# A hybrid model's layers on one core: the norm's weight and scale in one instruction behind the power, x's parts side by side, x loaded first, the first MLP chunk by token halves

## Chip, cores and metric

The kernel runs on one core of a Trainium2 chip. The metric is the device time of one execution in microseconds. TensorE (PE) multiplies matrices, VectorE (DVE), ScalarE (ACT) and GpSimd (POOL) work on rows of elements, SyncE (SP) and ACT issue most of the DMAs here. Each engine works through its instructions in the order in which they stand in its program, and waits on semaphores for the others.

## The reference, cut to what matters

```python
D_MODEL, SEQ, DEPTH, NORM_EPS = 1024, 256, 2, 1e-6

def rms_norm(x, w):
    xf = x.astype(jnp.float32)
    xf = xf * lax.rsqrt(jnp.mean(xf * xf, axis=-1, keepdims=True) + NORM_EPS)
    return (xf * w.astype(jnp.float32)).astype(x.dtype)
```

256 tokens of width 1024, all in fp32, pass through two layers, each a mixer (hgrn, dilated attention and a state-space part on slices of one projection) and a "peer" block (product keys choose experts), then an RG-LRU block, an MLP, a sparse-attention block (nsa), a second MLP, and a last norm. Each block is x + block(rms_norm(x, w)), and an MLP is `relu(x @ up)**2 @ down`. The change rewrites the norms, eight ahead of blocks and one at the end.

## The kernel before, in words

The residual x stays in SBUF as two token halves (t = 0, 1) of 128 partitions by 1024, each worked on in two column halves (`HALVES`, j = 0, 1). Every weight chunk of 512 KB (128x1024, fp32) is loaded into a tile `raw` (`load`, L258, SP's queue) and split by `chunk` into two fp32r parts, `hi` (a cast on ACT, L271) and `lo` (raw - hi on DVE, L273). The normed activations are split in the same way into `xh` and `xl`, the two parts of a tile `xx`. A product takes three matmuls: hi with xh, lo with xh, hi with xl. `feat_mm` (L289) takes 256 columns (all tokens) at a time; its first call after a norm does all eight of the first kind, then the eight of the second, then the eight of the third. `feat_cat` (L295, L296), used in the MLPs from the second chunk on, takes hi with xh and xl as one operand of 512 columns, and lo with xh beside it with 256. `tok_mm` (L322) makes the sums with tokens as rows, into four PSUM tiles; its last matmuls (L353) and the additions into x (L356) go token half by token half.

The norm ahead of each block (`norm_T`) goes through these steps:
- `squares`: per token half two squares on ACT (L381) with their sums in `nss`.
- `normed`: per token half two DVE multiplies x * sqrt(D) * w (L390), then `ns` on DVE (L392, sum plus epsilon), its power -1/2 on POOL (L393), and two DVE scalings by it (L398). For t = 0 the output is the tile `norm`, for t = 1 `nxs`.
- eight transposes on PE for each token half (L428), four to a PSUM tile; casts of these to xh on ACT (L435); the subtractions that give xl on DVE (L420).
- keep-warm matmuls of ones (L310) between the transposes of the two halves, in every norm but the first.

A scheduler (the tile framework) orders each engine's instructions. `issue_after` tells it that an instruction is to be issued behind another one. `self.behind` holds such instructions for the next three chunks: hi of the first is issued behind the last square and its lo behind the last scaling, the next two behind the last cast (hi) and the last subtraction (lo).

At the start, ACT's queue loads x, and SP's queue loads the first norm's weights, broadcast to all partitions (512 KB), ahead of the first weight chunks. Functions of setup make small constants meanwhile.

Of the kernel before, what the change touches and what calls it, by code (L numbers as in the profile page):

```python
# [10 lines left out]
F32 = mybir.dt.float32  # L11
# [10 lines left out]
P = 128  # L22
S = 256
# [158 lines left out]
class K:  # L182


    def __init__(self, ctx, tc, a):
# [9 lines left out]
        self.added = self.summed = self.row = None  # L195
# [23 lines left out]
    def load_x(self, src):  # L219
        for t in range(NT):  # L220
            for js in HALVES:
                self.nc.scalar.dma_start(self.x[:, t, js], src[t * P:(t + 1) * P, js])
            if t == 0:
                self.row = self.norm_row("attn_norm", 0)
        self.nc.scalar.dma_start(self.ident, self.a["c_ident"])
# [53 lines left out]
    def feat_mm(self, ps, wh, wl, xh, xl, m=P, kc=KC):  # L279
# [8 lines left out]
        for i, (w, x, k) in enumerate(seq):  # L288
            nc.tensor.matmul(ps, w[:, k], x[:, k], start=i == 0, stop=i == len(seq) - 1)  # L289

    def feat_cat(self, ps, wh, wl, x2, kc=KC):

        nc = self.nc
        for k in range(kc):
            nc.tensor.matmul(ps, wh[:, k], x2[:, :, k], start=k == 0, stop=False)  # L295
            nc.tensor.matmul(ps[:, :S], wl[:, k], x2[:, 0, k], start=False, stop=k == kc - 1)  # L296

    def split_x(self, name):

        x2 = self.stream.tile([P, 2, KC, S], F32R, tag="x2", name=self.nm(name))  # L300
        return x2, x2[:, 0], x2[:, 1]
# [75 lines left out]
    def squares(self, t):  # L377

        ss = self.const.tile([P, 2], F32, tag="nss", name=self.nm("nss"), bufs=2)
        for j, js in enumerate(HALVES):  # L380
            last = self.nc.scalar.activation(self.bank("a"), self.x[:, t, js], AF.Square, accum_out=ss[:, j:j + 1])  # L381
        return ss, last

    def normed(self, t, ss, w, dst, between=lambda: None):
# [3 lines left out]

        for js in HALVES:
            ready = nc.vector.scalar_tensor_tensor(dst[:, js], self.x[:, t, js], math.sqrt(D), w[:, js], op0=OP.mult, op1=OP.mult)  # L390
        with self.issue_after(ready):
            last = nc.vector.scalar_tensor_tensor(r, ss[:, 0:1], D * EPS, ss[:, 1:2], op0=OP.add, op1=OP.add)  # L392
# [3 lines left out]
        with self.issue_after(last):  # L396
            for js in HALVES:
                last = nc.vector.tensor_scalar(dst[:, js], dst[:, js], r, None, op0=OP.mult)  # L398
        return last

    def norm_row(self, wname, wi):
# [4 lines left out]
        return w  # L406

    def norm_T(self, pool, wname, wi):

        nc = self.nc  # L410
        w, self.row = self.row if self.row is not None else self.norm_row(wname, wi), None
# [9 lines left out]

        for t in range(NT):
            sc = self.normed(t, sq[t][0], w, xs[t], (lambda: low(0)) if t else lambda: None)
# [7 lines left out]
            if t == 0 and self.summed is not None:  # L431

                self.keep_warm(4, tr, self.summed)
            for _, b, h in parts[2 * t:]:
                cp = nc.scalar.copy(h, b)  # L435
# [3 lines left out]
        self.behind = [(sq[1][1], sc), (cp, self.lows), (cp, self.lows)]  # L439
# [29 lines left out]
    def setup_first(self):  # L469
# [5 lines left out]
        nc.vector.tensor_tensor(t[:, 0:2], hl[:, 0:2], hl[:, 2:4], op=OP.max)  # L475
# [11 lines left out]
        nc.vector.tensor_scalar(self.cwh, self.cols[:, o:o + 70], 0.5, None, op0=OP.mult)  # L487
        self.qn = c.tile([P, 2], F32, name="qn8")
        nc.vector.tensor_scalar(self.qn, self.col("q_norm", 0, 2), 0.125, None, op0=OP.mult)
# [4 lines left out]
        nc.scalar.activation(self.nega, self.nega, AF.Exp)  # L494
# [8 lines left out]
        nc.tensor.matmul(b[:6, :384], rb, oh, start=True, stop=True)  # L503
# [671 lines left out]
    def setup_second(self):  # L1175
# [97 lines left out]
    def mlp(self, i):  # L1273
        nc, a, tc = self.nc, self.a, self.tc
        v3 = lambda t_: t_.rearrange("p (k m) -> p k m", k=KC)
        with tc.tile_pool(name=f"mlp{i}", bufs=3) as pool:
# [4 lines left out]
            def up(f):  # L1281
# [3 lines left out]
                if f == 0:  # L1285
                    self.feat_mm(b[:, :S], v3(wh), v3(wl), xh, xl)
# [323 lines left out]
```

## Time and profile before

| | us |
|---|---|
| three runs | 2548.58, 2551.44, 2552.85 |
| median | 2551.44 |
| profiled execution, time | 2545.15 |
| profiled execution, span of the core | 2543.4 |
| PE busy | 2493.9 |
| DVE busy | 1875.2 |
| ACT busy | 1230.2 |

The span goes from the first to the last instruction. The mean granted clock of PE over it is 0.991 of full speed. Busy times are sums over the span; engines work beside each other, so they say how full an engine is, not what the end waits for. The busy time of one matmul (0.28 us for 256 columns) overlaps with the next; from one start to the next is less.

### The profile page before, as it was taken

The page shows a single profiled execution, that of the slowest core. Times are in us where ns is not written, and L with a number is a line of the kernel's source. Part 1 is how long each engine was busy: PE and PEld are TensorE (multiplying, and loading weights), DVE is VectorE, ACT ScalarE, POOL GpSimd, SP SyncE. Part 2 cuts the span into 40 slices and gives each one's busy share as a digit, 9 for nine tenths or more (in the row PEclk, how much of TensorE's full clock was granted, in tenths as well). Part 3 has the DMA queues.
Part 4 walks back from the last instruction along what each step waited for, and adds up shares of the span by engine and source line. Part 5 has one row for each costly group of instructions (what it writes and reads, how often), then busy time and mean ns, then how long its engine had stood idle before and what let it go on. Part 6 is the DMA issues. An engine that isn't in the chain of part 4 may idle for free.

```text
span 2543.4 us, 42782 instructions
## 1 busy us (share of the span) xinstructions
PE 2493.9 (98%) x16984; PEld 2159.3 (85%) x16984; DVE 1875.2 (74%) x3309; ACT 1230.2 (48%) x1861; POOL 55.6 (2%) x70
## 2 busy tenths in 40 slices
PE   8999999999999998999999999999999999999998
PEld 6789999988878887889989988878889788886887
DVE  8769969965696557869969955696559766756666
ACT  5544454445534445544454345534447544455544
POOL 2000000000000003000000000000000000000000
PEclk9999999999999998999999999999999999999999
DMA  6334454455545555244554455545555455621554
GB/s 214 104 134 158 176 189 160 156 194 187 174 158 185 195 191 178 95 141 153 179 191 158 158 192 189 174 150 191 196 193 173 167 190 189 202 73 61 192 189 149
DMA packets 122065, 426.17 MB, mean 168 GB/s; under 512 B 14748, under 2 KB 18696, under 8 KB 121736
## 3 DMA queue, kind: packets, MB, share of 16 engines
q1 hardware_dynamic: 120856, 421.79, 48.4%
q8 instruction: 133, 2.18, 0.3%
q10 hardware_dynamic: 1008, 1.64, 0.2%
q14 instruction: 68, 0.56, 0.1%
HBM read 421.83 MB, written 2.24 MB: 167 GB/s over the span
## 4 chain that ended last, share of the span: by engine, by line
PE 82%; DVE 13%; ACT 2%; issue 1%; DMA 1%; POOL 0%; ACTq 0%; POOLq 0%; DVEq 0%
PE psacc L322 40%; PE psa L289 14%; PE psa L295 12%; PE psa L296 6%; DVE lo L273 4%; PE psg L1044 2%; PE psacc L289 2%; DVE tk L940 1%; PE psa L1474 1%; PE psacc L353 1%; DVE si L942 1%; DVE si L939 1%; DVE sv L941 1%; DVE sv L938 0%; PE psacc L428 0%
## 5 line engine op out<-in xcount | busy, mean ns | idle before, releaser
L271 ACT CAST hi<-raw 128x1024 fp32r<-128x1024 f32 (+1 forms) x778 | 811.0, 1045 | 919.8 <-PE psa L289 343.9
L273 DVE TENSOR_TENSOR lo<-raw,hi 128x1024 fp32r<-128x1024 f32 (+1 forms) x778 | 942.5, 1218 | 412.0 <-ACT hi L271 411.3
L289 PE MATMUL psa<-xx,hi 128*128 128x256 f32 x3328 | 602.5, 285 | 4.3 <-ACT xx L435 1.7
L289 PEld LDWEIGHTS psa<-xx,hi 128*128 128x128 f32 x3328 | 515.4, 192 | 8.0 <-ACT xx L435 3.6
L289 PE MATMUL psa<-xx,lo 128*128 128x256 f32 x1664 | 463.1, 284 | 2.0 <-DVE lo L273 1.9
L295 PE MATMUL psa<-xx,hi 128*128 128x512 f32 x1296 | 463.3, 400 | 0.5 <-ACT mr L1287 0.5
L296 PE MATMUL psa<-xx,lo 128*128 128x256 f32 x1296 | 362.7, 280 | 0.0
L289 PEld LDWEIGHTS psa<-xx,lo 128*128 128x128 f32 x1664 | 314.7, 192 | 5.2 <-DVE lo L273 4.6
L322 PE MATMUL psacc<-hi,ch 128*128 128x512 f32 x984 | 306.4, 392 | 0.1
L322 PE MATMUL psacc<-lo,ch 128*128 128x512 f32 x984 | 304.3, 390 | 0.0
L322 PE MATMUL psacc<-hi,cl 128*128 128x512 f32 x984 | 303.6, 389 | 0.3 <-DVE cl L1015 0.2
L295 PEld LDWEIGHTS psa<-xx,hi 128*128 128x128 f32 x1296 | 243.3, 188 | 63.9 <-DVE ca L971 3.8
L296 PEld LDWEIGHTS psa<-xx,lo 128*128 128x128 f32 x1296 | 244.6, 189 | 2.4
L322 PEld LDWEIGHTS psacc<-hi,cl 128*128 128x128 f32 x984 | 184.6, 188 | 40.1 <-DVE cl L1015 1.2
L322 PEld LDWEIGHTS psacc<-lo,ch 128*128 128x128 f32 x984 | 184.7, 188 | 38.7
L322 PEld LDWEIGHTS psacc<-hi,ch 128*128 128x128 f32 x984 | 182.6, 188 | 36.4
L1014 ACT CAST ch<-ca 128x512 fp32r<-128x512 f32 x124 | 76.9, 621 | 139.9 <-PE psacc L322 137.7
L1015 DVE TENSOR_TENSOR cl<-ca,ch 128x512 fp32r<-128x512 f32 x124 | 85.4, 690 | 58.3 <-ACT ch L1014 58.0
L1048 DVE TENSOR_TENSOR ca<-psg,ca 128x512 f32<-128x512 f32 x128 | 82.2, 683 | 16.5 <-PE psg L1044 15.1
L322 PE MATMUL psacc<-hi,xx 128*128 128x512 f32 (+1 forms) x320 | 86.0, 380 | 0.0
L1034 DVE TENSOR_TENSOR pg<-o,selg 128x1024 f16<-128x1024 f16 x128 | 82.4, 682 | 0.0
L322 PE MATMUL psacc<-hi,muh 128*128 128x512 f32 x248 | 78.9, 397 | 0.0
(411 smaller groups left out, 2796.6 us busy)
## 6 DMA issues: line engine op xcount, KB each, us to landing
raw<-in_down SPq DMA_DIRECT2D x256, 512.0 KB, 3.2
raw<-in_up SPq DMA_DIRECT2D x256, 512.0 KB, 3.2
raw<-in_mlp_up SPq DMA_DIRECT2D x64, 512.0 KB, 3.3
raw<-in_mlp_down SPq DMA_DIRECT2D x64, 512.0 KB, 3.3
raw<-in_w_in_t SPq DMA_DIRECT2D x32, 512.0 KB, 3.9
raw<-in_w_in_f SPq DMA_DIRECT2D x22, 512.0 KB, 3.8
raw<-in_w_out SPq DMA_DIRECT2D x16, 512.0 KB, 3.4
raw<-in_w_query SPq DMA_DIRECT2D x16, 512.0 KB, 3.2
```

Of the source, the lines that this page charges most:

```text
L271: nc.scalar.copy(hi, src)
L273: nc.vector.tensor_sub(lo, src, hi)
L289: nc.tensor.matmul(ps, w[:, k], x[:, k], start=i == 0, stop=i == len(seq) - 1)
L295: nc.tensor.matmul(ps, wh[:, k], x2[:, :, k], start=k == 0, stop=False)
L296: nc.tensor.matmul(ps[:, :S], wl[:, k], x2[:, 0, k], start=False, stop=k == kc - 1)
L322: nc.tensor.matmul(acc[t][n][:, :widths[n]], x[:, xs], w[:, off[n]:off[n] + widths[n]], start=first and i == 0, stop=last and i == len(seq ...
L353: self.summed = nc.tensor.matmul(acc[t][j], x_[:, ts_], w_[:, HALVES[j]], start=False, stop=w_ is wl)
L1014: nc.scalar.copy(ch.rearrange("p b t -> p (b t)"), src)
L1015: nc.vector.tensor_sub(cl.rearrange("p b t -> p (b t)"), src, ch.rearrange("p b t -> p (b t)"))
L1034: nc.vector.tensor_tensor(pairs(pg[:, i]), pairs(o1), twice(sg[:, i], 32), op=OP.mult)
L1044: nc.tensor.matmul(bk[:, tt * 64:(tt + 1) * 64], o2[:, tk], pg[:, i, tk], start=i == 0, stop=i == 1)
L1048: nc.vector.tensor_tensor(v, bk.rearrange("p (t i) -> p i t", t=8), v, op=OP.mult)
```

## The change

- `normed` takes the power first; then one DVE instruction per column half makes x * r * w. The squares are scaled by D^-0.5 in place of the factor sqrt(D). For t = 0 the second half is issued behind the last x add. ns of t = 1 is issued behind the multiplies of t = 0.
- All casts to xh are issued behind the last square. Three keep-warm matmuls stand in place of four. hi of the first chunk is issued behind the casts of t = 0.
- `xx` is laid out so that xh and xl of one k stand side by side.
- x is loaded first, t = 0 on SP's queue and t = 1 on ACT's; the first norm's weights come as one row of 1024, which two matmuls with ones spread over the partitions into PSUM (`first_weights`).
- The first chunk of an MLP runs as 48 matmuls of 128 columns (`feat_tiles`), one token half after the other.
- Setup work on DVE, ACT and PE is issued behind the last subtraction, or the last matmul of the first product (most of these places are left out below).

```diff
@@ -217,12 +217,22 @@
         return self.ps.tile([P, 512], F32, tag=tag, name=self.nm("ps" + tag), bufs=bufs)
 
     def load_x(self, src):
-        for t in range(NT):
+        nc = self.nc
+        for t, q in zip(range(NT), (nc.sync, nc.scalar)):
             for js in HALVES:
-                self.nc.scalar.dma_start(self.x[:, t, js], src[t * P:(t + 1) * P, js])
-            if t == 0:
-                self.row = self.norm_row("attn_norm", 0)
-        self.nc.scalar.dma_start(self.ident, self.a["c_ident"])
+                q.dma_start(self.x[:, t, js], src[t * P:(t + 1) * P, js])
+        self.first_row = self.wts.tile([P, D], F32, tag="raw", name="first_row", bufs=4)[0:1]
+        nc.scalar.dma_start(self.ident, self.a["c_ident"])
+        nc.scalar.dma_start(self.first_row, self.a["attn_norm"][0:1, :])
+
+    def first_weights(self):
+
+        w = []
+        for js in HALVES:
+            b = self.bank("acc", 4)
+            self.nc.tensor.matmul(b, self.ones[0:1, :P], self.first_row[:, js], start=True, stop=True)
+            w.append(b)
+        return w
 
     def rstd(self, pool, ss, n, width):
 
@@ -286,19 +296,27 @@
         else:
             seq = [(w, x, k) for k in range(kc) for w, x in ((wh, xh), (wh, xl), (wl, xh))]
         for i, (w, x, k) in enumerate(seq):
-            nc.tensor.matmul(ps, w[:, k], x[:, k], start=i == 0, stop=i == len(seq) - 1)
+            self.last_mm = nc.tensor.matmul(ps, w[:, k], x[:, k], start=i == 0, stop=i == len(seq) - 1)
+
+    def feat_tiles(self, ps, wh, wl, xh, xl, kc=KC):
+
+        for t in range(NT):
+            ts_ = slice(t * P, (t + 1) * P)
+            for w, x in ((wh, xh), (wl, xh), (wh, xl)):
+                for k in range(kc):
+                    self.nc.tensor.matmul(ps[:, ts_], w[:, k], x[:, k, ts_], start=w is wh and x is xh and k == 0, stop=x is xl and k == kc - 1)
 
     def feat_cat(self, ps, wh, wl, x2, kc=KC):
 
         nc = self.nc
         for k in range(kc):
-            nc.tensor.matmul(ps, wh[:, k], x2[:, :, k], start=k == 0, stop=False)
-            nc.tensor.matmul(ps[:, :S], wl[:, k], x2[:, 0, k], start=False, stop=k == kc - 1)
+            nc.tensor.matmul(ps, wh[:, k], x2[:, k], start=k == 0, stop=False)
+            nc.tensor.matmul(ps[:, :S], wl[:, k], x2[:, k, 0], start=False, stop=k == kc - 1)
 
     def split_x(self, name):
 
-        x2 = self.stream.tile([P, 2, KC, S], F32R, tag="x2", name=self.nm(name))
-        return x2, x2[:, 0], x2[:, 1]
+        x2 = self.stream.tile([P, KC, 2, S], F32R, tag="x2", name=self.nm(name))
+        return x2, x2[:, :, 0], x2[:, :, 1]
 
     def keep_warm(self, n, *after):
 
@@ -378,24 +396,23 @@
 
         ss = self.const.tile([P, 2], F32, tag="nss", name=self.nm("nss"), bufs=2)
         for j, js in enumerate(HALVES):
-            last = self.nc.scalar.activation(self.bank("a"), self.x[:, t, js], AF.Square, accum_out=ss[:, j:j + 1])
+            last = self.nc.scalar.activation(self.bank("a"), self.x[:, t, js], AF.Square, scale=D ** -0.5, accum_out=ss[:, j:j + 1])
         return ss, last
 
-    def normed(self, t, ss, w, dst, between=lambda: None):
+    def normed(self, t, ss, w, dst, between=lambda: None, behind=None):
 
         nc = self.nc
         r = self.const.tile([P, 1], F32, tag="ns1", name=self.nm("ns1"), bufs=2)
-
-        for js in HALVES:
-            ready = nc.vector.scalar_tensor_tensor(dst[:, js], self.x[:, t, js], math.sqrt(D), w[:, js], op0=OP.mult, op1=OP.mult)
-        with self.issue_after(ready):
-            last = nc.vector.scalar_tensor_tensor(r, ss[:, 0:1], D * EPS, ss[:, 1:2], op0=OP.add, op1=OP.add)
+        with self.issue_after(behind):
+            last = nc.vector.scalar_tensor_tensor(r, ss[:, 0:1], EPS, ss[:, 1:2], op0=OP.add, op1=OP.add)
         nc.gpsimd.tensor_tensor(r, r, self.mhalf[:, :1], op=OP.pow)
         with self.issue_after(last):
             last = between() or last
         with self.issue_after(last):
-            for js in HALVES:
-                last = nc.vector.tensor_scalar(dst[:, js], dst[:, js], r, None, op0=OP.mult)
+            for j, js in enumerate(HALVES):
+
+                with self.issue_after(self.added if j > t else None):
+                    last = nc.vector.scalar_tensor_tensor(dst[:, js], self.x[:, t, js], r, w[j], op0=OP.mult, op1=OP.mult)
         return last
 
     def norm_row(self, wname, wi):
@@ -403,12 +420,12 @@
         src = self.a[wname]
         w = self.wts.tile([P, D], F32, tag="raw", name=self.nm("nw"), bufs=4)
         self.nc.sync.dma_start(w, bass.AP(tensor=src.tensor, offset=src.offset + wi * D, ap=[[0, P], [1, D]]))
-        return w
+        return [w[:, js] for js in HALVES]
 
     def norm_T(self, pool, wname, wi):
 
         nc = self.nc
-        w, self.row = self.row if self.row is not None else self.norm_row(wname, wi), None
+        w = self.norm_row(wname, wi) if self.summed is not None else self.first_weights()
         xs = (self.norm0, pool.tile([P, NT, D], F32, tag="big", name=self.nm("nxs"), bufs=1)[:, 1])
         self.x2, xh, xl = self.split_x("xx")
 
@@ -419,8 +436,9 @@
             l, b, h = parts[i]
             return nc.vector.tensor_tensor(l, b, h, op=OP.subtract)
 
+        sc = None
         for t in range(NT):
-            sc = self.normed(t, sq[t][0], w, xs[t], (lambda: low(0)) if t else lambda: None)
+            sc = self.normed(t, sq[t][0], w, xs[t], (lambda: low(0)) if t else lambda: None, sc)
             for j in range(2):
                 b = self.bank("acc", 4)
                 for k in range(4):
@@ -430,13 +448,16 @@
                 parts.append((xl[d], b.rearrange("p (k t) -> p k t", k=4), xh[d]))
             if t == 0 and self.summed is not None:
 
-                self.keep_warm(4, tr, self.summed)
+                self.keep_warm(3, tr, self.summed)
             for _, b, h in parts[2 * t:]:
-                cp = nc.scalar.copy(h, b)
+                with self.issue_after(sq[1][1]):
+                    cp = nc.scalar.copy(h, b)
+            if t == 0:
+                cp0 = cp
         with self.issue_after(sc):
             for i in (2, 1, 3):
                 self.lows = low(i)
-        self.behind = [(sq[1][1], sc), (cp, self.lows), (cp, self.lows)]
+        self.behind = [(cp0, sc), (cp, self.lows), (cp, self.lows)]
         self.first_mm = True
         return xh, xl
 
...
@@ -500,7 +525,8 @@
         nc.sync.dma_start(rb, a["rel_bias"])
         nc.sync.dma_start(ra, a["c_rel_add"])
         b = self.bank("g")
-        nc.tensor.matmul(b[:6, :384], rb, oh, start=True, stop=True)
+        with self.issue_after(self.last_mm):
+            nc.tensor.matmul(b[:6, :384], rb, oh, start=True, stop=True)
         nc.vector.tensor_tensor(ra, ra, b[:6, :384], op=OP.add)
         dr = self.dram.tile([6, 384], F32, name="relb")
         nc.sync.dma_start(dr, ra)
@@ -1283,7 +1311,8 @@
                 wh, wl = self.chunk(a["mlp_up"][i, f])
                 r = pool.tile([P, S], F32, tag="mr", name=self.nm("mr"))
                 if f == 0:
-                    self.feat_mm(b[:, :S], v3(wh), v3(wl), xh, xl)
+                    self.first_mm = False
+                    self.feat_tiles(b[:, :S], v3(wh), v3(wl), xh, xl)
                     nc.scalar.copy(r, b[:, :S])
                 else:
                     self.feat_cat(b, v3(wh), v3(wl), self.x2)
@@ -1560,9 +1589,9 @@
         nc = self.nc
         w = self.norm_row("norm_final", 0)
         with self.tc.tile_pool(name="fin", bufs=1) as pool:
-            y = (self.norm0, pool.tile([P, D], F32, name="fy"))
+            y, last = (self.norm0, pool.tile([P, D], F32, name="fy")), None
             for t in range(NT):
-                self.normed(t, self.squares(t)[0], w, y[t])
+                last = self.normed(t, self.squares(t)[0], w, y[t], behind=last)
                 for js, q in zip(HALVES, (nc.sync, nc.scalar)):
                     q.dma_start(out[t * P:(t + 1) * P, js], y[t][:, js])
 
```

The first place is DVE's program in peer l=0, from the last multiply ahead of the power of token half 1 to lo of the first weight chunk. `xx<-psacc` are the four subtractions, `iota` and `irep` two small casts of the peer. Before:

```order
L390 SCALAR_TENSOR_TENSOR nxs_1839<-x_sb,nw_1837 128x512
L392 SCALAR_TENSOR_TENSOR ns_295_1875<-nss_1846 128x1
L420 TENSOR_TENSOR xx_1840<-psacc_1858,xx_1840 128x4x128
L398 TENSOR_SCALAR nxs_1839<-nxs_1839,ns_295_1875 128x512 x2
L420 TENSOR_TENSOR xx_1840<-psacc_1863,xx_1840 128x4x128
L273 TENSOR_TENSOR lo_1909<-raw_1906,hi_1908 128x1024
L420 TENSOR_TENSOR xx_1840<-psacc_1883,xx_1840 128x4x128
L420 TENSOR_TENSOR xx_1840<-psacc_1888,xx_1840 128x4x128
```

Now, from the multiply of the second column half of token half 0 (`norm`):

```order
L415 SCALAR_TENSOR_TENSOR norm_72<-x_sb,ns_292_1851,nw_1837 128x512
L407 SCALAR_TENSOR_TENSOR ns_296_1872<-nss_1846 128x1
L437 TENSOR_TENSOR xx_1840<-psacc_1856,xx_1840 128x4x128
L415 SCALAR_TENSOR_TENSOR nxs_1839<-x_sb,ns_296_1872,nw_1837 128x512 x2
L437 TENSOR_TENSOR xx_1840<-psacc_1861,xx_1840 128x4x128
L437 TENSOR_TENSOR xx_1840<-psacc_1878,xx_1840 128x4x128
L437 TENSOR_TENSOR xx_1840<-psacc_1883,xx_1840 128x4x128
L957 CAST iota_1893<-ii_1895 128x128
L958 CAST irep_1894<-ii_1895 128x256
L283 TENSOR_TENSOR lo_1904<-raw_1901,hi_1903 128x1024
```

The first lo stood behind two of the four subtractions and now stands behind all four and the two small casts; the multiplies (`norm`, `nxs`) stand behind the ns of their token half.

The second place is PE's program in the first MLP, from the transposes of its norm into the first chunks. `psa` is the sum of a chunk; the matmuls of 512 columns belong to the chunks behind the first. Before:

```order
L428 MATMUL psacc_21262<-ident_sb,norm_72 128x128 x4
L428 MATMUL psacc_21267<-ident_sb,norm_72 128x128 x4
L310 MATMUL psg_21272<-ones 128x256 x4
L428 MATMUL psacc_21287<-ident_sb,nxs_21243 128x128 x4
L428 MATMUL psacc_21292<-ident_sb,nxs_21243 128x128 x4
L289 MATMUL psa_21306<-xx_21244,hi_21309 128x256 x8
L289 MATMUL psa_21306<-xx_21244,lo_21310 128x256 x8
L289 MATMUL psa_21306<-xx_21244,hi_21309 128x256 x8
L295 MATMUL psa_21344<-xx_21244,hi_21347 128x512
```

Now:

```order
L446 MATMUL psacc_21240<-ident_sb,norm_72 128x128 x4
L446 MATMUL psacc_21245<-ident_sb,norm_72 128x128 x4
L328 MATMUL psg_21250<-ones 128x256 x3
L446 MATMUL psacc_21262<-ident_sb,nxs_21223 128x128 x4
L307 MATMUL psa_21281<-xx_21224,hi_21284 128x128
L446 MATMUL psacc_21267<-ident_sb,nxs_21223 128x128 x4
L307 MATMUL psa_21281<-xx_21224,hi_21284 128x128 x7
L313 MATMUL psa_21343<-xx_21224,hi_21346 128x512
L307 MATMUL psa_21281<-xx_21224,lo_21285 128x128 x8
L307 MATMUL psa_21281<-xx_21224,hi_21284 128x128 x16
L307 MATMUL psa_21281<-xx_21224,lo_21285 128x128 x8
L307 MATMUL psa_21281<-xx_21224,hi_21284 128x128 x8
```

The first chunk's 24 matmuls of 256 columns have become 48 of 128. One of them stands between the transposes of token half 1, and the next chunk's first matmul of 512 columns, which stood behind the first chunk, now stands ahead of its first lo.

## Rows read from the trace of the kernel before

**Rows 1.** Page of before, parts 1, 4 and 5 (columns named on the page).

```profile
PE 2493.9 (98%) x16984; PEld 2159.3 (85%) x16984; DVE 1875.2 (74%) x3309; ACT 1230.2 (48%) x1861; POOL 55.6 (2%) x70
...
PE 82%; DVE 13%; ACT 2%; issue 1%; DMA 1%; POOL 0%; ACTq 0%; POOLq 0%; DVEq 0%
...
L295 PE MATMUL psa<-xx,hi 128*128 128x512 f32 x1296 | 463.3, 400 | 0.5 <-ACT mr L1287 0.5
```

**Rows 2.** Timeline, peer l=0: start us, us, engine, operation, count, [idle before].

```profile
169.75 0.62 PE L322 MATMUL psacc<-hi,mm 128*128 128x512 f32 x2
...
171.11 0.40 PE L353 MATMUL psacc<-lo,mm 128*128 128x512 f32 x1
...
171.34 1.04 PE L428 MATMUL psacc<-ident_sb,norm 128*128 128x128 f32 x8
171.54 0.69 DVE L356 TENSOR_TENSOR x_sb<-x_sb,psacc 128x512 f32<-128x512 f32 x1
...
172.22 1.89 PE L310 MATMUL psg<-ones 128*128 128x256 f32 x8
172.27 0.69 DVE L390 SCALAR_TENSOR_TENSOR nxs<-x_sb,nw 128x512 f32<-128x512 f32 x1
172.46 0.61 ACT L381 ACTIVATE psa<-x_sb 128x512 f32<-128x512 f32 x1
...
173.22 0.16 DVE L392 SCALAR_TENSOR_TENSOR ns<-nss 128x1 f32<-128x1 f32 x1 [0.26 <-ACT psa L381]
...
174.06 0.88 DVE L398 TENSOR_SCALAR nxs<-nxs,ns 128x512 f32<-128x512 f32 x2
...
174.60 1.09 PE L428 MATMUL psacc<-ident_sb,nxs 128*128 128x128 f32 x8 [0.49 <-DVE nxs L398]
...
175.29 1.07 ACT L435 CAST xx<-psacc 128x512 fp32r<-128x512 f32 x2 [0.68 <-PE psacc L428]
175.45 1.21 DVE L273 TENSOR_TENSOR lo<-raw,hi 128x1024 fp32r<-128x1024 f32 x1
...
175.93 1.23 PE L289 MATMUL psa<-xx,hi 128*128 128x256 f32 x8 [0.24 <-ACT xx L435]
...
176.59 1.28 DVE L420 TENSOR_TENSOR xx<-psacc,xx 128x512 fp32r<-128x512 f32 x2
...
177.00 1.12 PE L289 MATMUL psa<-xx,lo 128*128 128x256 f32 x8
...
177.96 1.60 PE L289 MATMUL psa<-xx,hi 128*128 128x256 f32 x12
```

**Rows 3.** Timeline, first MLP, its first chunks (columns as above).

```profile
2008.78 0.50 PE L295 MATMUL psa<-xx,hi 128*128 128x512 f32 x1 [0.23 <-ACT mr L1287]
...
2009.25 0.39 PE L295 MATMUL psa<-xx,hi 128*128 128x512 f32 x1
...
2011.36 0.40 PE L295 MATMUL psa<-xx,hi 128*128 128x512 f32 x1
```

**Rows 4.** Timeline of PE, first MLP, twelve down matmuls (six rows).

```profile
2098.20 0.64 PE L322 MATMUL psacc<-hi,muh 128*128 128x512 f32 x2
...
2100.98 0.39 PE L295 MATMUL psa<-xx,hi 128*128 128x512 f32 x1
```

**Rows 5.** Timeline, nsa's norm.

```profile
2186.54 1.29 DVE L390 SCALAR_TENSOR_TENSOR nxs<-x_sb,nw 128x512 f32<-128x512 f32 x2
...
2187.74 0.15 DVE L392 SCALAR_TENSOR_TENSOR ns<-nss 128x1 f32<-128x1 f32 x1
```

**Rows 6.** Timeline, start of the kernel.

```profile
10.39 0.60 ACT L381 ACTIVATE psa<-x_sb 128x512 f32<-128x512 f32 x1 [1.27 <-DMA x_sb<-in_x]
...
18.04 1.66 PE L289 MATMUL psa<-xx,hi 128*128 128x256 f32 x8
```

**Rows 7.** Timeline of PE, rglru's sum into x.

```profile
1977.33 0.73 PE L322 MATMUL psacc<-lo,mm 128*128 128x512 f32 x2 [1.55 <-DVE lo L273]
```

**Rows 8.** Windows: stretch, its length, busy of each engine, PEclk, DMA share, GB/s.

```profile
1978.30:1981.70 3.40, 3.40 (x10) 2.62 (x9) 3.40 (x5) 0.93 (x3) 0.00 (x0) 0.50 0.45 159
```

More of the change, by code (lines that the diff above doesn't have):

```diff
@@ L194, in __init__ @@
         self.behind = []
-        self.added = self.summed = self.row = None
+        self.added = self.summed = None
         self.first_mm = False
@@ L474, in setup_first @@
         t = c.tile([P, 12], F32, name="lbt")
-        nc.vector.tensor_tensor(t[:, 0:2], hl[:, 0:2], hl[:, 2:4], op=OP.max)
+        with self.issue_after(self.lows):
+            nc.vector.tensor_tensor(t[:, 0:2], hl[:, 0:2], hl[:, 2:4], op=OP.max)
         nc.vector.tensor_tensor(t[:, 2:4], hl[:, 0:2], t[:, 0:2], op=OP.subtract)
@@ L486, in setup_first @@
         self.cwh = c.tile([P, 70], F32, name="cwh")
-        nc.vector.tensor_scalar(self.cwh, self.cols[:, o:o + 70], 0.5, None, op0=OP.mult)
+        with self.issue_after(self.lows):
+            nc.vector.tensor_scalar(self.cwh, self.cols[:, o:o + 70], 0.5, None, op0=OP.mult)
         self.qn = c.tile([P, 2], F32, name="qn8")
-        nc.vector.tensor_scalar(self.qn, self.col("q_norm", 0, 2), 0.125, None, op0=OP.mult)
+        with self.issue_after(self.lows):
+            nc.vector.tensor_scalar(self.qn, self.col("q_norm", 0, 2), 0.125, None, op0=OP.mult)
         self.nega = c.tile([P, DEPTH, 6], F32, name="nega")
@@ L493, in setup_first @@
         nc.sync.dma_start(self.nega.rearrange("p l h -> p (l h)"), bass.AP(tensor=al.tensor, offset=al.offset, ap=[[0, P], [1, DEPTH * 6]]))
-        nc.scalar.activation(self.nega, self.nega, AF.Exp)
+        with self.issue_after(self.lows):
+            nc.scalar.activation(self.nega, self.nega, AF.Exp)
         nc.vector.tensor_scalar(self.nega, self.nega, -1.0, None, op0=OP.mult)
@@ L1178, in setup_second @@
         self.rgh = c.tile([P, 16], F32, name="rgh")
-        nc.vector.tensor_scalar(self.rgh, self.col("rg_b_a", 0, 16), 0.5, None, op0=OP.mult)
+        with self.issue_after(self.lows):
+            nc.vector.tensor_scalar(self.rgh, self.col("rg_b_a", 0, 16), 0.5, None, op0=OP.mult)
         nl = c.tile([P, 8], F32, name="nl")
-        nc.vector.tensor_scalar(nl, self.col("rg_lam", 0, 8), -1.0, None, op0=OP.mult)
+        with self.issue_after(self.lows):
+            nc.vector.tensor_scalar(nl, self.col("rg_lam", 0, 8), -1.0, None, op0=OP.mult)
         sp = self.softplus(c, nl, P, 8, "lm")
```

## Prediction

> **What bounds the kernel now.** I read the page first: busy times, then the chain that ended last. TensorE (PE) is busy 98% of the span and carries 82% of that chain, VectorE (DVE) 13% [rows 1]. So three things can move the time: how long the matmuls take, how many there are, and the few places where PE stands still. Work taken from DVE, ScalarE (ACT) or a queue counts only where PE waits for it.
>
> Next I read the timeline of one norm stage, peer l=0, whose pattern the stages repeat [rows 2]. Look at PE alone. After the last matmul of the old sum (171.11) it transposes token half 0 at once, runs the keep-warm matmuls from 172.22, is idle 0.49 before the transposes of half 1 (174.60) and 0.24 before the first eight weight matmuls (175.93). From there it never stops: lo x8 at 177.00, hi at 177.96. It can go on because DVE wrote lo of the first weight chunk at 175.45 to 176.66, ahead of the two last subtractions (176.59). A stage therefore costs only 0.73 us of PE idle time. That is all that a faster norm could win there, and what an operation put ahead of that lo would lose.
>
> **The change, part by part.**
>
> *Norm in one instruction.* Two operations per 512 columns (0.69 ahead of the power, then 0.88 for two behind it) become one of 0.69 behind the power [rows 2]. DVE is spared some 0.45 us per half; PE sees none of that by itself. The path behind the power gets longer: two multiplies of 0.69 run at 1.29 a pair [rows 5], where two scalings took 0.88. Followed through peer l=0, all from [rows 2]:
> 1. The last x add runs 171.54 to 172.23; the second half of token half 0 is multiplied only behind it, to about 172.85. Its four transposes, which ran at 171.8, start at 172.9. This is covered by the keep-warm matmuls, three now: 1.89/4 x 3 = 1.4 us from 173.35, to 174.75.
> 2. The last square no longer stands behind a cast: 172.27 instead of 172.46. So ns comes at 173.03 (0.76 behind it, as before) and the power's result at 173.87 (0.84 behind ns, as for the scaling at 174.06).
> 3. The first cast, moved behind the squares, runs 172.95 to 173.55. DVE's order has the subtraction that needs it (0.69 with its wait, to 174.2) between ns and the multiplies, which therefore run 174.13 to 174.82 and to 175.44, not 174.06 to 174.94. The transposes of half 1 start at 174.9 and 175.5, where all eight had started at 174.60.
> 4. The last cast began 1.17 after those eight began (two in 1.07 from 175.29). It now begins about 0.69 behind 175.50, at 176.19, and ends at 176.78. The last subtraction ends at 177.5.
> 5. In the new order lo of the first chunk stands behind all the subtractions, not ahead of two. It runs 177.45 to 178.67 (1.21), where it had ended at 176.66.
> 6. PE starts hi x8 at about 176.2 and stands still from 177.2. One or two matmuls of a later chunk are put in there; lo x8 starts at 178.75, not 177.00. The 24 matmuls of the chunk end 16 x 0.12 = 1.92 later, at 180.67. Before it was 177.96 + 8 x 0.12 = 178.92. The loss is 1.75, less 0.12 to 0.24 for the matmuls put in, plus two small casts that stand ahead of lo in the peers alone: **1.7 us**, taken for the four stages attention l=1, peer l=0, peer l=1 and rglru: **+6.8**.
>
> In nsa, the second MLP and the final norm the chain is longer before: two multiplies (1.29) held up ns until 2187.74 [rows 5], and they are gone. But the new order puts the first multiply, which waits for the power, ahead of the last x add, which costs some 0.5 of the 1.1 us won. So nsa loses 1.7 - 0.6 = **+1.1**, and the end gains about **-0.2** (two multiplies of 1.29 for two scalings of 0.88, on a chain that starts 0.6 earlier).
>
> *First MLP chunk by token halves.* 24 matmuls of 256 columns at 0.12 become 48 of 128. No such matmul of this type is in the trace. The nearest row by shape is the transposes: 128 columns, eight from 171.34 to 172.22, 0.11 each [rows 2]. Eight of the 48 run ahead while PE would wait. On the clock of [rows 2], the other 40 start when lo is there (178.67) and take 4.4 us, to 183.1; the next chunk's first 512-column matmul is done by then. Before, PE started that matmul at 178.92, was busy with it for 0.39 and then idle for 0.23, until the first chunk's sum had been copied out [rows 3], to 179.54. That gives **+3.5** for the first MLP. The second begins as nsa does and has the 0.6 back, less some delay of the first copy: 3.5 - 0.5 = **+3.0**.
>
> Bounds for the 128-column matmul: 256 columns take 0.120 and 512 take 0.227 (six from 169.75 to 171.11 [rows 2]), so a fixed 0.013 and 0.42 ns a column, which makes 0.067: 40 x 0.043 = 1.7 less per MLP, 3.4 in all. The keep-warm matmuls, plain fp32 of 256 columns, took 1.89/8 = 0.22 per record or less than half a matmul; at that rate 128 columns cost up to 0.22: 4.4 more per MLP, 8.8 in all. I take 0.11, since a 128-column stationary operand is loaded for each in both.
>
> The Trainium skill ("TensorE: Matmul & The Clock Gate", section "Back-to-back issue gap") has another value: a stream of weight load and matmul is spaced by both, about 81 ns at 128 columns. By it, an estimate, 40 matmuls take 3.2 us and the two MLPs lose 2.3 us less, so the sum below would be about 9.2 instead of 11.5. The transposes here do not agree, but no run so far shows the very operation.
>
> *x's parts side by side.* The 512-column operand of a pair (L295) becomes contiguous. A pair takes 0.352 (six from 2009.25 to 2011.36 [rows 3]); the sum of the undisturbed rows is 0.227 + 0.120 = 0.347. If the split is the reason for the difference, 1296 pairs [rows 1] x 0.0047 = 6 us. But the down matmuls, whose operands are contiguous already, are also slow in the MLPs: 12 in 2.78, 0.232 each [rows 4], against 0.227 in the peer's sum. A split operand can't explain those directly, so the slowness seems to come from something else in these stages. I take nothing; the bound is under the rivals.
>
> *The start.* The weights row of 512 KB no longer shares the first transfers with x, and two queues carry x. Before, the last halves of x had arrived at 10.39 and PE began at 18.04 with weights, eight of them busy for 1.66 us [rows 6] where a later stage shows 1.23 [rows 2]. One megabyte of x without the half megabyte beside it should have arrived by about 7, two thirds of 10.39, which is 3.4 sooner or, with loads of weights still beside it, 2; against this stand two new broadcast matmuls on PE and the longer multiplies, and for it the half clock, which the earlier matmuls may escape (8 x 0.06). I estimate **-2.7**, between -1.5 and -4. The setup work moved behind the norm is hidden: nothing waits for it for tens of us.
>
> **Sum:** 6.8 + 1.1 + 3.5 + 3.0 - 2.7 - 0.2 = **+11.5 us**. The profiled execution took 2545.15 us (span 2543.4), 6.3 less than the median of 2551.44, which I put down to the spread of executions. On it the change gives 2556.7; on the median 2563. A measurement of this kernel can tell about 0.2% (5 us) from no change, so this is slower.
>
> **Rivals.**
> - *x's layout pays (ends on the other side).* Place: L295 and what follows it in both MLPs. If pairs fall to 0.347 and the slowness that follows them goes too (768 down matmuls x 0.005 = 4), it gives 10 us, net +1.5: 2553, no change. It decides from 6.5 us up. For it: the disturbed matmuls sit only where pairs run. Against: matmuls of contiguous operands share it. Chance 0.24.
> - *The stages do what they say.* PE's stalls turn out short, as the transposes and casts come sooner than I work out, and lo of the first chunk is not late; 128 columns go at 0.067. Then the stages cost nothing, the MLPs 48 x 0.067 - 24 x 0.12 = 0.3 each in place of 6.5, and start and end give 2.9: net -2.3, or 2549; with the start's far end -3.6, and past 0.2% from where the layout returns 2 us beside it: 2546. Against it: DVE works in order, and lo stands behind three subtractions that wait for casts. Chance 0.2.
> - *The clock falls.* PE will stand still about 1.4 us in one go behind hi x8. PE was idle for 1.55 us ahead of 1977.33 [rows 7], and the stretch from 1978.30 then has a granted clock of 0.50 [rows 8], half of 2.4 GHz: 3.4 us, of which 1.7 are lost. In up to six stages that is 10 us: 2573. Against: a stage's stall is a little shorter, and matmuls stand close to it on both sides. Chance 0.08.
> - *128 columns at the slow bound:* +8.8: 2572. Chance 0.08.
>
> **How the numbers follow.** My own case has 0.40, 2557 to 2569, its width from start (1.3 each way), pitch (-3.4) and the second mixer, whose matmul order the change also shuffles (I allow 2 to 4 us either way). With the clock and the slow bound, slower by over 0.2% has 0.50. The layout's case lies mostly within 0.2%, with the low end of my own: same 0.28. Faster 0.22: the second rival, and the layout with a short pitch. The range reaches from the second rival, 2545, to the slow bound, 2573.
>
> **What would show it.** Right: PE idle some 1.4 us between hi x8 and lo x8 of a stage's first chunk, ended by DVE lo; that lo behind the last subtraction; 48 matmuls of 128 columns at about 0.11 in each MLP; the pair still at 0.352; the first weight matmul near 14 to 15 us. Wrong: a pair at 0.347 or below, or lo of the first chunk ready before hi x8 ends.

## The result, and the profile after

The changed kernel takes 2578.80 us (median of 6 runs, 2576.41 to 2583.11) against 2552.14 for the kernel before run beside it: ratio 1.011, 95% interval 1.0095 to 1.0125. A second set of runs gave 2579.05 against 2549.24: 1.0111 (1.0094 to 1.0128). It is slower, as forecast, but by 27 to 30 us and not by 11.5, and above the range's end of 2573.

The page of the changed kernel, parts 1 and 4 (columns as in [rows 1]; lines of its code stand 10 to 29 further down):

```profile
span 2574.6 us, 42813 instructions
...
PE 2517.7 (98%) x17022; PEld 2176.4 (85%) x17022; DVE 1865.0 (72%) x3273; ACT 1231.7 (48%) x1861; POOL 57.3 (2%) x70
...
PE 85%; DVE 10%; ACT 2%; DMA 1%; issue 1%; POOL 0%; SPq 0%; DVEq 0%; POOLq 0%; ACTq 0%
```

DVE is spared 10 us, which is worth nothing; PE is busy 24 us longer with nearly the same matmuls. That points at matmuls that have become slower, not at idle time alone. The next view, windows of the changed kernel cut at the last x add of each block, says where (stretch, length, busy of PE, PEld, DVE, ACT, POOL, then PEclk, DMA share, GB/s). The rows are first mixer, first peer, second mixer, rglru, first and second MLP:

```profile
0.00:178.07 178.07, 164.43 (x1268) 134.33 (x1269) 125.63 (x262) 88.69 (x174) 25.04 (x32) 0.93 0.41 138
178.07:969.45 791.38, 787.62 (x5502) 693.88 (x5501) 598.09 (x1050) 362.88 (x457) 1.11 (x2) 1.00 0.51 177
969.45:1132.69 163.24, 149.24 (x1244) 123.97 (x1243) 114.17 (x233) 86.51 (x166) 25.08 (x25) 0.95 0.37 125
...
1924.18:2016.40 92.22, 87.04 (x600) 79.76 (x599) 75.96 (x111) 63.08 (x104) 1.10 (x2) 0.98 0.50 166
2016.40:2209.53 193.13, 190.38 (x950) 160.34 (x948) 121.26 (x173) 90.79 (x142) 1.10 (x2) 0.97 0.51 177
...
2374.48:2567.62 193.14, 190.58 (x950) 160.56 (x950) 121.23 (x175) 90.33 (x140) 1.10 (x2) 0.97 0.49 169
```

The first MLP in the same cut of before, at full clock throughout:

```profile
2000.73:2185.14 184.41, 183.36 (x928) 153.56 (x926) 120.78 (x175) 90.33 (x140) 0.59 (x2) 1.00 0.54 186
```

All blocks beside the same cut of the profile of before, with the stretches at half clock (granted 0.5, 1.2 of 2.4 GHz) summed up for each:

| block | before us | half | changed us | half | longer by | forecast |
|---|---|---|---|---|---|---|
| first mixer with the start | 171.54 | 13.65 | 178.07 | 23.89 | 6.5 | -2.7 |
| first peer | 789.73 | 0 | 791.38 | 0 | 1.65 | 1.7 |
| second mixer | 159.03 | 13.65 | 163.24 | 17.07 | 4.2 | 1.7 |
| second peer | 789.77 | 0 | 791.49 | 0 | 1.7 | 1.7 |
| rglru | 90.66 | 3.41 | 92.22 | 3.41 | 1.6 | 1.7 |
| first MLP | 184.41 | 0 | 193.13 | 10.24 | 8.7 | 3.5 |
| nsa | 165.08 | 10.24 | 164.95 | 6.83 | -0.1 | 1.1 |
| second MLP | 185.37 | 0 | 193.14 | 10.24 | 7.8 | 3.0 |
| last norm | 7.81 | 5.31 | 6.98 | 4.45 | -0.8 | -0.2 |

In the peers and rglru, where the clock is the same in both, the forecast holds to 0.15 us. In the MLPs and mixers it does not, and there the clock differs too. If a stretch at half clock costs half its length, the MLPs' forecasts and 10.24 / 2 make 8.6 and 8.1, close to the 8.7 and 7.8 measured. Each column is one execution, and that of before was a fast one (2545.15): in the first mixer another run with the same order of matmuls (e3 below) had 27.3 us at half, so the 6.5 there is partly chance.

The timeline of the changed kernel in peer l=0 answers to [rows 2]:

```profile
178.07 0.69 DVE L374 TENSOR_TENSOR x_sb<-x_sb,psacc 128x512 f32<-128x512 f32 x1 [0.43 <-PE psacc L371]
...
178.67 0.75 DVE L415 SCALAR_TENSOR_TENSOR norm<-x_sb,ns,nw 128x512 f32<-128x512 f32 x1
...
179.47 0.66 PE L446 MATMUL psacc<-ident_sb,norm 128*128 128x128 f32 x4 [1.00 <-DVE norm L415]
...
180.69 1.40 DVE L415 SCALAR_TENSOR_TENSOR nxs<-x_sb,ns,nw 128x512 f32<-128x512 f32 x2
181.48 1.32 PE L446 MATMUL psacc<-ident_sb,nxs 128*128 128x128 f32 x8
182.01 2.14 DVE L437 TENSOR_TENSOR xx<-psacc,xx 128x512 fp32r<-128x512 f32 x3
...
182.81 1.40 PE L299 MATMUL psa<-xx,hi 128*128 128x256 f32 x8
...
184.40 3.49 DVE L283 TENSOR_TENSOR lo<-raw,hi 128x1024 fp32r<-128x1024 f32 x3
185.37 0.51 PE L299 MATMUL psa<-xx,hi 128*128 128x256 f32 x2 [1.15 <-ACT hi L281]
185.71 1.18 PE L299 MATMUL psa<-xx,lo 128*128 128x256 f32 x8
```

Read it from the last x add, which stands 6.53 later than in before: hi x8 at 4.74 behind it (4.39 before), lo x8 at 7.64 (5.46 before). DVE has no idle time from 182.01 to 187.9: three subtractions, two small casts, then lo. PE stands still 1.00 us ahead of the second four transposes and 1.15 ahead of two matmuls of a later chunk, which the scheduler pulled in ahead of lo; their hi (ACT) ends the wait at 185.37, and lo x8 follows 0.34 later.

In the first MLP the late lo makes a like stall, in two parts (0.89 and 0.42), and something else follows. The timeline of the changed kernel there, which answers to [rows 3]:

```profile
2020.89 0.97 PE L307 MATMUL psa<-xx,hi 128*128 128x128 f32 x7
...
2022.75 0.50 PE L313 MATMUL psa<-xx,hi 128*128 128x512 f32 x1 [0.89 <-ACT hi L281]
2023.66 1.67 PE L307 MATMUL psa<-xx,lo 128*128 128x128 f32 x8 [0.42 <-DVE lo L283]
...
2025.13 3.62 PE L307 MATMUL psa<-xx,hi 128*128 128x128 f32 x16
...
2028.55 1.91 PE L307 MATMUL psa<-xx,lo 128*128 128x128 f32 x8
2030.25 1.91 PE L307 MATMUL psa<-xx,hi 128*128 128x128 f32 x8
```

and its windows from the stall to the end of the chunk:

```profile
2020.60:2024.00 3.40, 2.09 (x15) 1.64 (x16) 3.30 (x5) 2.97 (x4) 0.00 (x0) 1.00 0.43 154
2024.00:2034.30 10.30, 10.30 (x47) 10.01 (x47) 3.06 (x4) 1.62 (x3) 0.00 (x0) 0.50 0.46 154
```

PE had been busy 2.09 of 3.40 us when the clock fell; then eight matmuls take 1.70 us (2028.55 to 2030.25), 0.21 each.

### The profile page after: what moved, and what is told of

It is laid out like the page before. It is cut to its first block, busy times and chain, and to the rows that moved or that the text cites. A ratio compares the mean times of both kernels' runs of the same rounds, so it can differ in the third digit from the quotient of the medians.

```text
span 2574.6 us, 42813 instructions
## 1 busy us (share of the span) xinstructions
PE 2517.7 (98%) x17022; PEld 2176.4 (85%) x17022; DVE 1865.0 (72%) x3273; ACT 1231.7 (48%) x1861; POOL 57.3 (2%) x70
## 3 DMA queue, kind: packets, MB, share of 16 engines
HBM read 421.31 MB, written 2.24 MB: 165 GB/s over the span
## 4 chain that ended last, share of the span: by engine, by line
PE 85%; DVE 10%; ACT 2%; DMA 1%; issue 1%; POOL 0%; SPq 0%; DVEq 0%; POOLq 0%; ACTq 0%
PE psacc L340 39%; PE psa L299 16%; PE psa L313 12%; PE psa L314 6%; DVE lo L283 3%; PE psg L1070 2%; PE psacc L299 2%; DMA raw<-in_w_in_t 1%; PE psacc L371 1%; PE psa L1503 1%; PE psa L307 1%; ACT hi L281 1%; DVE tk L966 1%; PE psg L299 1%; PE psg L1521 0%
```

## Experiments

Two theories for the MLPs: A, the 128-column matmuls alone bring the clock down; B, the longer stall of the norm does. Later C: lo's late place in DVE's order costs, wherever it stands; D: the norm's longer path behind the power does.

**e1, the first chunk with 256 columns again** (the changed kernel, one edit):

```diff
-                    self.first_mm = False
-                    self.feat_tiles(b[:, :S], v3(wh), v3(wl), xh, xl)
+                    self.feat_mm(b[:, :S], v3(wh), v3(wl), xh, xl)
```

> The changed kernel with the first MLP chunk back at 24 matmuls of 256 columns. Theory A (the 128-column matmuls make the clock fall, as they keep PE too little busy): no stretch of half clock behind either MLP norm; each MLP stage costs what rglru's does, some 1.6 us over before, not 8.7 and 7.8; the whole about 13 us less than the changed kernel, near 2565. Theory B (the longer stalls of the norm make it fall): the half-clock stretch of 10 us stays in both MLPs, only 2 x 2.3 us of matmul time come back, near 2574.

**e2, these 24 matmuls twice** (e1 with `self.first_mm = True` and a second `feat_mm` behind the first, into the same sum):

> As the run before, but the first MLP chunk's 24 matmuls of 256 columns are done twice into the same sum, so that PE has 48 matmuls there as in the changed kernel, with the same order, stalls and nearly the same length, and only the columns differ. Theory A: no half clock in the MLPs, each 2.9 us longer than without the repeat, near 2571. Theory B: half clock of some 7 to 10 us in both, near 2580.

**e3, the kernel before with `feat_tiles` alone** (e1's edit the other way round, on the kernel before):

> The kernel before with the 128-column first MLP chunk alone: the short stalls of before, 128 columns. Theory A: the clock falls in both MLPs, each some 2.3 + 5 us longer, near 2566. Theory B: no fall, 2.3 us each, near 2557. If both are needed, also 2557.

**e4, the changed kernel with lo first:** the last two subtractions are issued behind the first chunk's lo.

```diff
         with self.issue_after(sc):
-            for i in (2, 1, 3):
-                self.lows = low(i)
+            low(1)
+        self.late = [lambda: low(2), lambda: low(3)]
...
         with self.issue_after(la):
-            nc.vector.tensor_sub(lo, src, hi)
+            lo_ins = nc.vector.tensor_sub(lo, src, hi)
+        for low in self.late:
+            with self.issue_after(lo_ins):
+                self.lows = low()
+        self.late = []
```

> The changed kernel with lo of the first chunk put ahead of the last two subtractions of xl, as before, and the 128-column chunk kept. Its stall ahead of the lo matmuls should shrink from about 1.15 to 0.5 or less: peers and rglru each 1.0 to 1.5 us shorter, nsa and the second mixer too. Theory A: the half clock in the MLPs stays, the whole 7 to 9 us less than the changed kernel, near 2571. Theory B: the fall goes with the stall, 17 to 19 us less, near 2561.

**e5, the kernel before with lo late**, and **e6, the same with the 128-column chunk**:

```diff
-        self.behind = [(sq[1][1], sc), (cp, self.lows), (cp, self.lows)]
+        self.behind = [(sq[1][1], self.lows), (cp, self.lows), (cp, self.lows)]
```

> The kernel before, with one change: lo of the first chunk is issued behind the last subtraction of xl, as it comes out in the changed kernel. The norm itself is as before. Theory C (it is lo's place that costs, by the stall ahead of the lo matmuls, and by the order of the second mixer's short matmuls, which the scheduler then lays out anew, nearly as in the changed kernel): peers and rglru 1.2 to 1.7 us longer each, nsa and the MLPs 1.2 to 2, the second mixer 4 to 10 with more half clock than 13.65 us; the whole near 2564. Theory D (it is the norm's longer path behind the power): within 3 us of before, and the second mixer as before.

> As the run before, with the 128-column first MLP chunk too. If the clock falls in the MLPs where short matmuls and a late lo come together, 10 us of half clock in both MLPs, each 8 us over before, the whole near 2577. If the fall also needs the changed norm's idle time ahead of its second four transposes, no half clock there, and the whole near 2568.

**e7, the kernel before with the changed start** (`load_x`, `first_weights` and the setup edits of the diff):

> The kernel before with the changed start alone: x first on two queues, one row of weights spread by PE, setup work behind the first norm. The order of PE differs from before in the first mixer only. If the start's gain comes through, first weights 2.2 us earlier and the whole 1 to 3 us faster, near 2549. If the first mixer takes it back (its short matmuls, a fall of the clock), the whole is within 2 us of before.

**e8, e4 with e1's edit:**

> The changed kernel with both costs taken away: lo of the first chunk ahead of the last two subtractions, and 256 columns in the first MLP chunk. What is left is the norm in one instruction, x's layout and the start. Theory C: MLPs within 0.5 us of before, the whole 2 us or more under the version with lo first alone, 2551 to 2554: no gain left from the norm. If the norm in one instruction, the layout (2 us by the pairs) or the start are worth something together, below 2549.

**e9, the changed kernel with PE kept busy in the MLP's stall:**

```diff
+                if t == 0 and w is wh and x is xh:
+                    self.keep_warm(3, mm)
```

> The changed kernel with three matmuls of ones between hi x8 and lo x8 of the first MLP chunk, where PE stands still for 0.9 and 0.4 us; the rest of PE's order is as changed. The stall's length is kept, only PE is busy in it. If the fall of the clock in the MLPs comes from idle time together with the short matmuls, it is gone (0 us of half clock in the MLPs), each MLP 4 to 5 us shorter, the whole near 2569. If the late lo costs by another way, or short matmuls alone keep the clock down, half clock of 7 to 10 us stays in the MLPs and the whole near 2578.

**e10, e4's edit in the second mixer's norm alone**, and **e11, in every norm but the mixers'** (`if wname == "attn_norm" and wi == 1` and `if wname != "attn_norm"` around it):

> The changed kernel with lo of the first chunk ahead of the last two subtractions in the norm of the second mixer alone. PE's order there is then that of the kernel before, but for three rows. If the second mixer's loss is the stall of its norm and the new order of its short matmuls: that stage within 1.5 us of before at 13.65 us of half clock, and the whole 4 to 8 us less than the changed kernel, near 2573. If the order there doesn't matter, only the stall of 1.2 to 1.6 us comes back, near 2577.

> The changed kernel with lo of the first chunk ahead of the last two subtractions in every norm but those of the two mixers (PE's order is the changed kernel's in the mixers and the lo-first version's elsewhere). The lo-first version took 2556.6. If the extra half clock outside the MLPs belongs to the mixers with a late lo, the whole is 8 to 12 us above it, 2564 to 2568, with a mean granted clock of 0.986 to 0.988. If the mixers lose only the stall, 2 x 1.5 us, near 2559 and a clock of 0.990.

**e12, the changed kernel again:**

> The changed kernel once more, for a second profile and more times. If the fall of the clock in the MLPs is there in every execution, 10 us of half clock in both MLPs again; if it depends on where the stall happens to fall, one of them may be without. The whole near 2579, clock 0.984.

What was measured ("over": median less that of the kernel before run beside it; clock: mean over the runs; half: us at half clock in the two MLPs of the profile). The kernel before had a mean clock of 0.9894 in 65 runs.

| run | lo | first MLP chunk | us | over | ratio, interval | clock | half |
|---|---|---|---|---|---|---|---|
| e1 | late | 24 x 256 | 2569.58 | 18.5 | 1.0066 (1.0047 to 1.0086) | 0.9862 | 0, 0 |
| e2 | late | 48 x 256 | 2574.56 | 23.5 | 1.009 (1.0073 to 1.0107) | 0.9858 | 0, 0 |
| e3 | early | 48 x 128 | 2553.37 | 2.3 | 1.0016 (1.0007 to 1.0025) | 0.9900 | 0, 0 |
| e4 | early | 48 x 128 | 2556.64 | 5.5 | 1.0028 (1.0017 to 1.0038) | 0.9899 | 0, 0 |
| e5 | late | 24 x 256 | 2565.15 | 16.0 | 1.007 (1.0057 to 1.0083) | 0.9873 | 0, 0 |
| e6 | late | 48 x 128 | 2577.63 | 28.4 | 1.0116 (1.0096 to 1.0135) | 0.9835 | 13.65, 0 |
| e7 | early | 24 x 256 | 2551.12 | 1.9 | 1.0009 (0.9998 to 1.002) | 0.9890 | 0, 0 |
| e8 | early | 24 x 256 | 2552.77 | 3.6 | 1.0014 (1.0005 to 1.0023) | 0.9892 | 0, 0 |
| e9 | late | 48 x 128, ones | 2574.55 | 23.7 | 1.0097 (1.0078 to 1.0117) | 0.9852 | 0, 0 |
| e10 | early in mixer 2 | 48 x 128 | 2574.65 | 23.8 | 1.0089 (1.007 to 1.0107) | 0.9853 | 13.65, 10.24 |
| e11 | late in mixers | 48 x 128 | 2563.92 | 14.7 | 1.0057 (1.0042 to 1.0073) | 0.9865 | 0, 0 |
| e12 | late | 48 x 128 | 2579.05 | 29.8 | 1.0111 (1.0094 to 1.0128) | 0.9838 | 10.24, 6.83 |

**Neither A nor B alone: the clock falls in the MLPs where a late lo and the 128-column chunk come together.** Short matmuls with the stall short or filled (e3, e4, e9, e11) and a late lo without short matmuls (e1, e2, e5) had no half clock in any of 14 MLPs. Together (the changed kernel, e6, e10, e12) they had it in 7 of 8. The times of all runs say the same: on the kernel before, the 128-column chunk costs 2.3 us with lo early (e3) and 12.5 with lo late (from e5 to e6), and in the second case the mean clock goes from 0.9873 to 0.9835, some 20 us more at half, or 10 lost.

Why it takes both is only partly shown. e2 has the same number of matmuls in nearly the same order as the changed kernel, but not the same stall: eight hi matmuls of 256 columns end later, and PE then stands still 0.20 and 0.41 us, not 0.89 and 0.42. (e1 is alike; e5 has 0.20 and 0.52.) So 128 columns do two things, lengthen the idle time ahead of lo and shorten the matmuls behind it, and no run here has a stall as long in an MLP with 256 columns behind it. The nearest are the peers: with lo late PE stands still there 1.15 us in one go, with 256 columns behind it, and none of 16 peer stages (two each in the changed kernel, e1, e2, e5, e6, e9, e10 and e12) has half clock. That speaks for the columns behind the stall, but does not prove it. The timeline of e2 in its first MLP:

```profile
2029.43 1.41 PE L299 MATMUL psa<-xx,hi 128*128 128x256 f32 x8
2031.04 0.51 PE L313 MATMUL psa<-xx,hi 128*128 128x512 f32 x1 [0.20 <-ACT hi L281]
2031.95 1.22 PE L299 MATMUL psa<-xx,lo 128*128 128x256 f32 x8 [0.41 <-DVE lo L283]
2033.01 2.08 PE L299 MATMUL psa<-xx,hi 128*128 128x256 f32 x16
2034.93 1.12 PE L299 MATMUL psa<-xx,lo 128*128 128x256 f32 x8
2035.89 1.12 PE L299 MATMUL psa<-xx,hi 128*128 128x256 f32 x8
```

From lo on, the 40 matmuls take 4.9 us (2031.95 to 2035.89 + 8 x 0.12); the 128-column ones took 8.3 (2023.66 to 2030.25 + 1.70). e9 tries the stall's part: with ones in it, the clock stays up in both MLPs of its profile. From hi x7 to lo x8 it still takes 2.77 us (2019.67 to 2022.44; 2020.89 to 2023.66 in the changed kernel), but PE stands still only 0.45 of it. One more thing moved: the next chunk's matmul of 512 columns, pulled in ahead of lo in the changed kernel, stands behind the chunk again. The timeline in the first MLP:

```profile
2019.67 0.98 PE L307 MATMUL psa<-xx,hi 128*128 128x128 f32 x7
2020.48 1.51 PE L330 MATMUL psg<-ones 128*128 128x256 f32 x6
2022.44 1.11 PE L307 MATMUL psa<-xx,lo 128*128 128x128 f32 x8 [0.45 <-DVE lo L283]
2023.39 1.95 PE L307 MATMUL psa<-xx,hi 128*128 128x128 f32 x16
2025.17 1.06 PE L307 MATMUL psa<-xx,lo 128*128 128x128 f32 x8
2026.07 1.06 PE L307 MATMUL psa<-xx,hi 128*128 128x128 f32 x8
```

At full clock eight take 0.90 (2025.17 to 2026.07). The median of e9 fell by 4, not by the 9 expected. Its profile is of the fastest of its four runs (2568.84); the others took 2574.45 to 2576.10 at a clock of 0.984 or 0.985, and whether the clock stayed up in their MLPs is not shown.

**C, not D.** e5 changes nothing but lo's place in the kernel before and loses 16.0 us (some 5 of them by the clock, 0.9873 against 0.9894); adding the 128-column chunk makes 28.4 (e6), the whole loss. With lo early, the norm in one instruction, x's layout and the start together lose 3.6 (e8), and the 128-column chunk 1.9 more (e4). So the norm's longer path (D) costs at most a few us. The timeline of e5 in peer l=0, with the old norm, has the changed kernel's stall to the hundredth:

```profile
180.00 1.23 PE L289 MATMUL psa<-xx,hi 128*128 128x256 f32 x8 [0.24 <-ACT xx L435]
181.52 3.49 DVE L273 TENSOR_TENSOR lo<-raw,hi 128x1024 fp32r<-128x1024 f32 x3
182.38 0.50 PE L289 MATMUL psa<-xx,hi 128*128 128x256 f32 x2 [1.15 <-ACT hi L271]
182.79 1.22 PE L289 MATMUL psa<-xx,lo 128*128 128x256 f32 x8
```

and that of e4, with the new norm and lo early, has none behind hi x8:

```profile
180.77 1.21 DVE L286 TENSOR_TENSOR lo<-raw,hi 128x1024 fp32r<-128x1024 f32 x1
180.98 1.41 PE L306 MATMUL psa<-xx,hi 128*128 128x256 f32 x8
181.91 1.28 DVE L444 TENSOR_TENSOR xx<-psacc,xx 128x512 fp32r<-128x512 f32 x2
182.22 1.12 PE L306 MATMUL psa<-xx,lo 128*128 128x256 f32 x8
```

**The mixers.** e11 puts lo late in the two mixers alone and loses 9 us against e4, at a clock of 0.9865 against 0.9899: 2 x 0.0034 x 2564 = 17 us more at half, up to 9 us. So more than their two stalls of some 1.5 us is lost there, at the low end of what was expected. The same shows in e1 and e2: they took 4.6 and 3.6 us more than theory A gave them, with no half clock in the MLPs but 61 and 68 us in the two mixers (27 in before). Why is open. With lo late the scheduler lays the second mixer's matmuls out anew (1440 lines added or taken out in PE's order against before; 6 in e4 and e10). But e10, which has nearly the order of before there, still showed 20.48 us at half in its one profile, 4.5 us over before and not within the 1.5 expected, and so did e7. One profile each does not tell which stretch falls more often.

**The start** (e7) moves the first weight matmul from 18.04 [rows 6] to 17.41 (2.2 us were expected), and it is at 15.85 in the changed kernel, with the norm in one instruction; yet nothing is left at the end. Rows of the changed kernel:

```profile
5.99 0.60 ACT L399 ACTIVATE psa<-x_sb 128x512 f32<-128x512 f32 x1 [0.56 <-DMA x_sb<-in_x]
...
9.26 1.98 PE L233 MATMUL psacc<-first_row,ones 1*128 1x512 f32 x4
...
10.49 1.54 DVE L415 SCALAR_TENSOR_TENSOR norm<-x_sb,ns,psacc 128x512 f32<-128x512 f32 x2 [2.24 <-PE psacc L233]
...
18.82 1.12 PE L299 MATMUL psa<-xx,lo 128*128 128x256 f32 x8
```

and the first lo of before:

```profile
19.54 1.12 PE L289 MATMUL psa<-xx,lo 128*128 128x256 f32 x8
```

The squares wait for x until 5.99, where it was 10.39 in before. But DVE's first multiply then waits 2.24 us for the weights, which PE spreads only from 9.26. And lo is late in the first mixer too: hi x8 comes 2.19 us sooner, lo x8 only 0.72. Later in the mixer DVE is busy 29.7 of the 30 us from 30 to 60 in before and 28.9 in the changed kernel; three windows of before:

```profile
30.00:40.00 10.00, 9.36 (x43) 7.38 (x41) 9.70 (x24) 6.70 (x8) 0.21 (x1) 1.00 0.98 352
40.00:50.00 10.00, 7.61 (x30) 5.73 (x30) 10.00 (x10) 5.04 (x10) 9.83 (x10) 0.83 0.50 176
50.00:60.00 10.00, 8.70 (x40) 6.48 (x40) 9.96 (x11) 7.22 (x11) 7.35 (x6) 1.00 0.46 160
```

DVE, not x's arrival, seems to set the pace in that stretch; that was read from the rows and not tried by itself.

## Why the prediction was wrong

- **The direction and the steps 1 to 6 held.** 1.7 us a stage was forecast; peers and rglru lost 1.56 to 1.72. Step 6 put lo x8 7.21 us behind the last x add, and it came at 7.64. The idle time in the peers was 1.15 and not 1.4, and the pulled-in chunk's hi ended it just ahead of lo. e4 and e5 show lo's place as the cause.
- **"The clock falls" is the step that failed.** It stood as a rival of chance 0.08, on the ground that the stall is a little shorter than one that was followed by half clock and that matmuls stand close to it. In the peers that held. In the MLPs the matmuls behind the stall are the 128-column ones. The sum counted these at full clock, and the rivals priced a fall of the clock and slow columns apart, never one by the other. It should have been asked what PE does just behind the stall. The rival's size was wrong too: it gave each of six stages 3.4 us at half, and two MLPs had 6.8 to 13.7 where they fell. By mean clocks (0.9837 and 0.9894) the changed kernel runs 84 us at half, the one before 54: 30 us, some 15 of the 27 to 30 lost. In the profiles two thirds of this lie in the MLPs (20.5 of 29.9 us), the rest, on balance, in the mixers. The remainder, 12 to 15, is close to the 11.5 of the sum, though not every term of it was right.
- **The second mixer was mis-sized.** 1.7 and an allowance of 2 to 4 were given; the two profiles of the changed kernel show 4.2 and 10.3 (159.03 against 163.24 and 169.29), with 3.4 and 17.1 us more at half. The clock's rival had 2563 and 10, the 2573 at which the range ends; by the runs the 10 had to be some 15.
- **The start's -2.7 did not come.** e7 took 1.9 us more (0.9998 to 1.002), so a gain above 0.5 us is unlikely. x did arrive early, but the two broadcast matmuls, named without a price, held the first multiply back. And the sum left out the late lo in the first mixer: of the 2.19 us won at the first hi, 0.72 are left at the first lo.
- **nsa** measured -0.1 for +1.1, with 3.4 us less at half: some 1.6 more at the same clock.
- **128 columns at 0.11 was right** at full clock: 0.90/8 = 0.11. In e3, 48 of them without the stall cost 1.8 us per MLP in the profile, less than 2.3. The Trainium skill's 81 ns ("TensorE: Matmul & The Clock Gate", "Back-to-back issue gap") did not show in this stream.
- **x's layout gives nothing, as taken.** Over the 1217 to 1226 pairs at full clock in each profile, a pair takes 0.352 on average from start to start in before and 0.351 in e7 and e5 with the old layout, 0.351 in the changed kernel and 0.352 in e1 with the new (pairs under 0.4 us).

No version here beats the kernel before. The start alone (e7) comes closest, at 0.09% over, which is not clear of no change; e8 is 0.14% slower.

## What to carry to other kernels

When an edit shifts a cast or an add, look at which operand the next matmuls wait for and where its producer now stands in its engine's order; here that one place was worth 16 us. A stall and a stretch of short matmuls may each be cheap and together halve the clock for what follows, so price them together: shortening the stall (e4) took the fall away, and filling it with ones (e9) did in the one profile. Short matmuls ahead of a wait also make it longer for PE (0.61 us with 256 columns, 1.31 with 128). And tell one profile's clock from the change's: two runs with the same order of matmuls in the first mixer (before and e3) had 13.65 and 27.3 us at half.

## What was not expected of the hardware

- The spread of one kernel's times is mostly the clock: in one set of runs, those of the kernel before at 0.991 took 2544.84 to 2546.69 us, the one at 0.987 2556.73. The clock alone, half of 2 x 0.004 x 2550, makes 10 of these 10 to 12 us.
- With 128 columns, half clock doubles the time of a matmul (0.21 against 0.11). PEld (weight loads) is then busy 10.01 of 10.30 us, and 4.00 of 4.00 in the same stretch of e9 at full clock (2022.80 to 2026.80). The weight loads may thus set the pace at either clock; no run tries it.
